# Two token tiles taken together in the mixing stage of a two-layer hybrid decoder trunk

## The chip, the cores and the metric

The kernel runs on one core of a Trainium2 chip. The metric is the device time of one launch in microseconds; a time is given as the median of several runs. A profiled execution of the same program gives a trace: when each instruction started on each engine, and what it waited for. The engines are TensorE (PE in the rows; its weight loads are PEld), VectorE (DVE), ScalarE (ACT), GpSimd (POOL) and SyncE (SP, which issues transfers).

## The reference

The input `x` has 256 tokens of width 1024. Two layers follow each other, each of this form:

```
h    = rms_norm(x, attn_norm)
proj = h @ w_in                       # 1024 x 3218
# split into three groups of heads, all causal:
#  retention: 6 heads of 64, rope on q and k, decay matrix in chunks of 128,
#             rms_norm per head, times silu(gate)
#  sparse attention: 6 query heads on 2 key/value heads, three branches:
#     compressed: 15 blocks of 32 tokens, every 16 tokens:
#         flat   = (tokens of the block + cmp_pe).reshape(32 * 64)
#         k_cmp  = rms_norm(gelu(flat_k @ cmp_w1[0]) @ cmp_w2[0])
#         v_cmp  = gelu(flat_v @ cmp_w1[1]) @ cmp_w2[1]
#     selected blocks, and a window; each branch has softmax with a T5 bias
#     and a sigmoid gate
#  gating: gelu, rms_norm per head, a causal 128 x 128 product over tokens
x = x + concat(heads) @ w_out
h = rms_norm(x, ffn_norm)
x = x + (silu(h @ w_gate) * (h @ w_up)) @ w_down       # inner width 2816
```

Everything is float32. The part that matters here is the per-head work between `proj` and `w_out`, and in it the compressed branch: for keys and for values, on 2 heads, a first layer that contracts 32 positions x 64 channels into 64, a GELU, and a second layer of 64 x 64.

## The kernel before

**Tiles.** The 256 tokens are two tiles of 128 (`t` = 0, 1), with tokens on the partitions. Weights stream from memory in pieces of up to 128 x 1024 (`PIECES`), in the order of use. Each fp32 product of the large matrices is made from three products: `stream_hi` has ACT cast a piece to a high half (`whi`), `stream_lo` has DVE subtract it to get a low half (`wlo`), and PE multiplies high by high, high by low and low by high. Activations are split in the same way after a transpose on PE (`hcat`, `Kh`/`Kl`, `Q`, and others).

**Stages of a layer.** `project` multiplies by the seven column chunks of `w_in` in the order `ORDER` (nk, nq, gm, nv, rq, rk, rg), and forks for each a handler `mix_nk`, `mix_nq` and so on, which works on the two result banks, one per token tile. `residual` multiplies by `w_out`; `project` and `project_t` make the FFN's first layer in chunks; `residual` again makes the second.

**Order of the work.** `Desk` is a planner that runs while the program is built. Handlers are generators: each yields an instruction with an engine, waits for events, or asks for a buffer from a pool (`w2k`: six of 128 x 512, `w1k`: four of 128 x 256, `sm` and `acc`: four PSUM banks each). The planner holds a time for each engine and a cost for each instruction (`_cost_PE`, `_cost_DVE`, `_cost_ACT`, `_cost_POOL`), takes the next by readiness and priority, and so fixes the order of every engine's queue. On the chip each engine runs its queue in that order, and waits on semaphores where a result is not there. A list of instructions that a handler yields at once stays together in the queue.

**The parts that the change touches.** `head_rms` computes per-head sums of squares of one tile and `rsqrt` their inverse root by small DVE operations (with `newton_only` eleven of them, otherwise two ACT functions and three DVE operations). `nk_tile`, `nq_tile`, `gm_tile` and `ret_norm` do this for each tile apart. `keys_twice` writes the normalized keys twice next to each other, `keys` turns them on PE (two transposes per tile) and splits them into `Kh` and `Kl`. `qk_transposed` turns the retention's queries and keys, one tile at a time. `ffn_first` turns the FFN's first chunk, two transposes per tile, and `row_scale` has one matmul per tile.

For the compressed branch `cmp_dup` writes the tokens twice next to each other, so that a transpose gives 128 partitions with the same 64 channels twice (two transposes per tile, and for keys and values apart); `cmp_tokens` has DVE copy even and odd positions to the lower and the upper 64 partitions of `aT`. `compress` then makes the first layer from 16 pairs of positions, for keys and for values, with 128 rows each:

```
PE.matmul(ph[64*j : 64*j+64, :33], self.w1[:, j, a, :], self.aT[:, j, a : a+257 : 8], ...)
for a in range(16) for j in range(2)
```

Here the weights (64 columns) stand in the array and 33 columns stream: 32 blocks, and a 33rd column with the position encoding `cmp_pe`, whose product is added to the others afterwards. After the GELU two products with `w2` follow apart from each other (`pv`, then `pk`). `load_layer` issues the loads of `w1`, `w2` and others on SP's queue; `ev_cmp` tells `compress` that they are there.

Of the kernel before, what the change touches and what calls it, by code (L numbers as in the profile page):

```python
# [22 lines left out]
NB = 384  # L23
# [132 lines left out]
FIRST, SLOT, GRAIN = 16512, 32, 512  # L156
# [33 lines left out]
class Engine:  # L190
# [209 lines left out]
class Trunk:  # L400
    def __init__(self, ctx, tc, x, wts, cst, oh, relb, par, w1, w2, wsT, out):
# [19 lines left out]
        self.pad(FIRST)  # L421
# [25 lines left out]
    def pad(self, first):  # L447

        gap = -(first + self.kept) % GRAIN
        if gap:  # L450
            self.fixed(f"pad{self.kept}", [128, gap // 4])
# [10 lines left out]
    def rsqrt(self, a, name, newton_only=False):  # L462
# [4 lines left out]
        z = self.tiny(name + "_z", shape)  # L467
        if newton_only:
            i = self.tiny(name + "_i", shape, I32)
            yield V.tensor_single_scalar(i, a.bitcast(I32), 1, op=ALU.logical_shift_right)  # L470
            yield V.tensor_scalar(y.bitcast(I32), i, -1.0, float(0x5F3759DF), op0=ALU.mult, op1=ALU.add)
        else:
            yield A.activation(z, a, AF.Ln)
            yield A.activation(y, z, AF.Exp, scale=-0.5)
        for _ in range(3 if newton_only else 1):
            yield V.scalar_tensor_tensor(z, y, -0.5, y, op0=ALU.mult, op1=ALU.mult)
            yield V.tensor_tensor(z, z, a, op=ALU.mult)
            yield V.scalar_tensor_tensor(y, z, 1.5, y, op0=ALU.add, op1=ALU.mult)
# [75 lines left out]
    def setup(self):  # L554
# [15 lines left out]
        self.w2 = self.fixed("w2", [128, 64])  # L570
        self.ev_cst, self.ev_bias, self.ev_scr = Event(), Event(), Event()
# [42 lines left out]
    def load_layer(self, l):  # L614
        SP, G = self.SP, self.G
        if l:
# [4 lines left out]
        w1 = lambda j: SP.dma_start(  # L621
            self.w1[:, j], self.d["w1"][l].rearrange("p (j a e) -> p j a e", j=2, a=16)[:, j], lat=False
        )
# [6 lines left out]
        if l:  # L630
# [4 lines left out]
            self.desk.fire(self.ev_cmp[l])  # L635
            yield causal()
            self.desk.fire(self.ev_lay[l])
            return
# [15 lines left out]
        self.desk.fire(self.ev_cmp[l])  # L654
        yield self.loaded[16]
        yield SP.dma_start(self.cst[:, C_DEC:], self.d["cst"][:, C_DEC:])
        self.desk.fire(self.ev_dec)

    def setup_bias(self):
# [7 lines left out]
        wide = self.tiny("rbw", [33, 6, n])  # L667
# [5 lines left out]
        yield PE.matmul(ps[: 6 * n, :NB], wide.rearrange("p h c -> p (h c)"), oh[:33, :NB], start=True, stop=True)  # L673
# [132 lines left out]
    def norm_scale(self):  # L806
# [21 lines left out]
        for op in ops:  # L828
            op.dur = self.desk.LAT["DVE"]
        yield ops  # L830
# [3 lines left out]
    def head_rms(self, src, nh, name, eps, newton_only=False):  # L834
        sq = yield Need(self.w2k)
        sv = sq[:, : nh * 64].rearrange("p (h d) -> p h d", h=nh)
        yield self.A.activation(sv, src, AF.Square)
        ss = self.tiny(name + "_ss", [128, nh])
        yield self.V.tensor_reduce(ss, sv, axis=AX.X, op=ALU.add)
        self.desk.give(self.w2k, sq)  # L840
        yield self.V.tensor_scalar(ss, ss, 1.0 / 64, eps, op0=ALU.mult, op1=ALU.add)
        r = yield from self.rsqrt(ss, name, newton_only)
        return r
# [9 lines left out]
    def mix_gm(self, l, ps):  # L853
        self.vn = self.gmv.rearrange("p (g t d) -> p t g d", g=4, t=2)
        both = [Event(), Event()]
        for t in range(2):
            self.desk.fork(self.gm_tile(l, t, ps[t], both[t]), 30)
        self.desk.fork(self.gm_mix(l, both), 30)

    def gm_tile(self, l, t, ps, ready):  # L860
        V, A, give = self.V, self.A, self.desk.give
        yield self.rready[t]
        self.z[t] = yield Need(self.w2k)
        z = self.z[t]
        yield A.activation(z, ps, AF.Gelu_apprx_tanh, scale=self.rstd[t])
        give(self.acc, ps)
        zv = self.heads(z[:, 256:], 4)
        r = yield from self.head_rms(zv, 4, f"gmr{t}", EPS, newton_only=True)
        yield V.tensor_tensor(self.vn[:, t], zv, r[:, :, None].to_broadcast([128, 4, 64]), op=ALU.mult)
        self.desk.fire(ready)  # L870
# [42 lines left out]
    def mix_nq(self, l, ps):  # L913
        for t in range(2):
            self.desk.fork(self.nq_tile(l, t, ps[t]), 10)

    def nq_tile(self, l, t, ps):
        V, A, give = self.V, self.A, self.desk.give
        yield self.rready[t]
        src = self.heads(ps, 8)  # L920
        r = yield from self.head_rms(src, 8, f"nqr{t}", self.axe[t])
        nn = yield Need(self.w2k)
        q = nn[:, :384]
        yield V.tensor_tensor(
            self.heads(q, 6), self.heads(ps[:, :384], 6), r[:, :6, None].to_broadcast([128, 6, 64]), op=ALU.mult
        )
        kk = yield from self.keys_twice(ps[:, 384:], r[:, 6:])
        give(self.acc, ps)
        pt = yield Need(self.sm)
        yield [self.transpose(pt[:, j * 128 : j * 128 + 128], q[:, j * 128 : j * 128 + 128]) for j in range(3)]  # L930
        give(self.w2k, nn)
# [3 lines left out]
        for g in range(2):  # L935
# [3 lines left out]
            yield A.activation(hi, src, AF.Copy, scale=self.qg[up])  # L939
            yield V.scalar_tensor_tensor(  # L940
                self.Q[low, hs, ts], src, self.qg[up], hi.bitcast(F32), op0=ALU.mult, op1=ALU.subtract
            )
        give(self.sm, pt)
        yield from self.keys(kk, 0, t)
        self.desk.fire(self.ev_nq[t])

    def keys_twice(self, src, r):
        kk = yield Need(self.w1k)
        yield self.V.tensor_tensor(
            kk.rearrange("p (g r d) -> p g r d", g=2, r=2),  # L950
# [3 lines left out]
        return kk  # L954

    def keys(self, kk, b, t):
        pt = yield Need(self.sm)
        yield [self.transpose(pt[:, g * 128 : g * 128 + 128], kk[:, g * 128 : g * 128 + 128]) for g in range(2)]
        self.desk.give(self.w1k, kk)
        src, gain = pt[:, :256].rearrange("p (g n) -> p g n", g=2), self.par[:, P_KG + 1 + b : P_KG + 2 + b]  # L960
        hi, lo = (k[:, :, b, t * 128 : t * 128 + 128] for k in (self.Kh, self.Kl))
# [4 lines left out]
    def mix_nk(self, l, ps):  # L966
        for t in range(2):
            left = [2]
            self.desk.fork(self.nk_tile(l, t, ps[t], left), 10)
            self.desk.fork(self.nk_rest(l, t, ps[t], left), 12)  # L970
# [6 lines left out]
    def nk_tile(self, l, t, ps, left):  # L977
        V, A, give = self.V, self.A, self.desk.give
        yield self.rready[t]
        src = self.heads(ps[:, :128], 2)  # L980
        r = yield from self.head_rms(src, 2, f"nkr{t}", self.axe[t])
        kk = yield from self.keys_twice(ps[:, :128], r)
        self.part_done(ps, left)
        yield from self.keys(kk, 1, t)
        self.desk.fire(self.ev_nk[t])

    def nk_rest(self, l, t, ps, left):
        yield self.rready[t]
        dup = yield from self.cmp_dup(ps[:, 384:512], t)
# [3 lines left out]
        yield from self.cmp_tokens(dup, 0, t)  # L993

    def cmp_dup(self, src, t):
        dup = yield Need(self.w1k)
        d4 = dup.rearrange("p (g r d) -> p g r d", g=2, r=2)
        yield [
# [851 lines left out]
```

## Time and profile before

| | |
|---|---|
| time, median of 3 runs | 630.7 us (630.62 to 630.87) |
| profiled execution | 630.12 us, of it span 628.3 us |
| PE busy | 623.6 us, 3628 instructions |
| DVE busy | 448.1 us, 976 instructions |
| ACT busy | 367.3 us, 685 instructions |
| POOL busy | 11.8 us, 25 instructions |
| granted TensorE clock | 0.999 |

The span runs from the first to the last instruction of the core; the profiled execution's own time is 1.8 us longer. PE busy time is the union of matmuls whose ends are modelled: a matmul's row can show 0.39 us while the next starts 0.23 us after it. So a cost on PE is read from start to start. Layer 0's mixing runs from about 26 to 110 us, layer 1's from about 330 to 418. A row of the timeline has the start in us, the length in us, the engine, the operation, the tile written and those read, the shapes, and how many instructions were merged into it. A row of a group by line ends with busy us, mean ns of one, idle us before them and what ended it. A row of a stretch has the busy us of PE, PEld, DVE, ACT and POOL with their counts, the granted clock, and the share and the rate of transfers.

### The profile page before, as it was taken

The numbers are of one execution on the slowest core, as the hardware profiler recorded it, in microseconds if no ns is written. First come the engines' busy times: TensorE is split into PE (matmuls) and PEld (weight loads), VectorE is DVE, ScalarE is ACT, GpSimd is POOL, SyncE is SP. The second block draws the span as 40 slices with busy tenths as digits, with TensorE's granted clock in tenths as the row PEclk, the third lists the DMA queues.
The fourth block names the chain that finished last, engine by engine and source line by source line (L and its number), as shares of the span: only waits on it lengthen the run. The fifth ranks groups of instructions, "written<-read, shape, count | busy, mean of one in ns | idle before, by whom it ended". The sixth has DMA issues, their size and how long they took to land.

```text
span 628.3 us, 9870 instructions
## 1 busy us (share of the span) xinstructions
PE 623.6 (99%) x3628; PEld 534.0 (85%) x3628; DVE 448.1 (71%) x976; ACT 367.3 (58%) x685; POOL 11.8 (2%) x25
## 2 busy tenths in 40 slices
PE   9999999999999999999999999999999999999998
PEld 7888788888898888888888978888889898888886
DVE  5988997685668586854388899867847777676432
ACT  6869854575555555544368885546755565555330
POOL 1120000000000000200000000000000000000000
PEclk9999999999999999999999999999999999999999
DMA  8884254355646556785356523545554656657631
GB/s 314 294 274 156 75 160 158 110 171 168 206 163 213 189 171 205 242 271 186 87 168 212 195 71 98 169 135 167 191 178 150 213 173 195 207 168 230 203 103 67
DMA packets 33887, 111.62 MB, mean 178 GB/s; under 512 B 4323, under 2 KB 5603, under 8 KB 33840
## 3 DMA queue, kind: packets, MB, share of 16 engines
q1 hardware_dynamic: 33520, 110.62, 54.0%
q8 instruction: 28, 0.46, 0.3%
q0 software_dynamic: 176, 0.36, 0.2%
q14 instruction: 19, 0.16, 0.1%
q10 hardware_dynamic: 144, 0.03, 0.0%
HBM read 109.64 MB, written 1.35 MB: 177 GB/s over the span
## 4 chain that ended last, share of the span: by engine, by line
PE 98%; DMA 1%; SPq 0%; ACT 0%; DVE 0%; issue 0%
PE acc L203 69%; PE sm L203 29%; DMA wst<-in_wts_dram 1%; SPq L203 0%; ACT whi L203 0%; DVE x L203 0%
## 5 line engine op out<-in xcount | busy, mean ns | idle before, releaser
L203 ACT CAST whi<-wst 128x1024 fp32r<-128x1024 f32 (+3 forms) x198 | 201.6, 1022 | 160.8 <-DMA wst<-in_wts_dram 97.0
L203 DVE TENSOR_TENSOR wlo<-wst,whi 128x1024 fp32r<-128x1024 f32 (+3 forms) x198 | 232.7, 1186 | 78.1 <-ACT whi L203 67.5
L203 PE MATMUL acc<-whi,hcat 128*128 128x512 f32 (+2 forms) x512 | 141.8, 380 | 0.1
L203 PEld LDWEIGHTS acc<-whi,hcat 128*128 128x128 f32 x512 | 91.3, 188 | 14.6 <-ACT whi L203 0.5
L203 PE MATMUL acc<-hcat,whi 128*128 128x512 f32 x320 | 99.4, 391 | 0.0
L203 PE MATMUL sm<-hcat,whi 128*128 128x512 f32 x320 | 98.8, 390 | 0.0
L203 PE MATMUL acc<-wlo,hcat 128*128 128x512 f32 (+2 forms) x256 | 79.4, 377 | 0.0
L203 PEld LDWEIGHTS sm<-hcat,whi 128*128 128x128 f32 x320 | 59.9, 188 | 12.6
L203 PEld LDWEIGHTS acc<-hcat,whi 128*128 128x128 f32 x320 | 58.9, 188 | 11.1
L203 PE MATMUL sm<-hcat,wlo 128*128 128x256 f32 x320 | 64.5, 283 | 0.0
L203 PE MATMUL acc<-hcat,wlo 128*128 128x256 f32 x320 | 64.3, 283 | 0.0
L203 PEld LDWEIGHTS acc<-wlo,hcat 128*128 128x128 f32 x256 | 46.8, 188 | 7.7 <-ACT hcat L203 0.6
L203 PEld LDWEIGHTS acc<-hcat,wlo 128*128 128x128 f32 x320 | 51.2, 191 | 1.6
L203 PE MATMUL acc<-whi,ah 128*128 128x512 f32 (+1 forms) x176 | 50.0, 378 | 0.0
L203 PE MATMUL acc<-whi,al 128*128 128x512 f32 (+1 forms) x176 | 50.0, 378 | 0.0
L203 DVE TENSOR_TENSOR w2k<-sm,w2k 128x256 f32<-128x256 f32 x40 | 16.9, 423 | 46.3 <-ACT w2k L203 46.3
L203 PE MATMUL acc<-wlo,ah 128*128 128x512 f32 (+1 forms) x176 | 49.9, 377 | 0.0
L203 PEld LDWEIGHTS sm<-hcat,wlo 128*128 128x128 f32 x320 | 49.9, 192 | 0.0
L203 PEld LDWEIGHTS acc<-whi,al 128*128 128x128 f32 x176 | 31.8, 188 | 5.6
L203 PEld LDWEIGHTS acc<-wlo,ah 128*128 128x128 f32 x176 | 31.8, 188 | 5.5
L203 PEld LDWEIGHTS acc<-whi,ah 128*128 128x128 f32 x176 | 31.7, 188 | 5.4
L203 ACT ACTIVATE hcat<-sm,par 128x128 fp32r<-128x128 f32 (+1 forms) x60 | 18.0, 384 | 10.1 <-PE sm L203 10.1
(213 smaller groups left out, 726.6 us busy)
## 6 DMA issues: line engine op xcount, KB each, us to landing
wst<-in_wts_dram SPq DMA_DIRECT2D x177, 512.0 KB, 4.2
PT<-in_wts_dram SPq DMA_DIRECT2D x7, 512.0 KB, 7.1
wst<-in_wts_dram SPq DMA_DIRECT2D x8, 384.0 KB, 3.0
w<-in_w_dram SPq DMA_DIRECT2D x4, 512.0 KB, 7.7
wst<-in_wts_dram SPq DMA_DIRECT2D x7, 256.0 KB, 2.9
wst<-in_wts_dram SPq DMA_DIRECT2D x4, 411.0 KB, 6.3
x<-in_x_dram SPq DMA_DIRECT2D x4, 256.0 KB, 5.2
B<-scr SPq DMA_DIRECT2D x4, 192.0 KB, 3.7
```

The lines of the kernel that those rows point to most:

```text
L203: return Op(self.name, lambda: fn(*a, **k), dur, table, lat, prio, banks)
```

## The change

Both token tiles go through the small operations together, and the compressed branch's first layer is laid out anew.

- `head_rms` takes both tiles: it makes sums for both into one small tile, and `rsqrt` works on both at once. `chain` yields small DVE operations as one list.
- `nk_tiles`, `nq_tiles`, `gm_tiles` and `ret_norm` replace the versions per tile. `keys` turns both tiles with four transposes in one list into one bank and splits them by one ACT and one DVE operation. `qk_transposed` turns four blocks at a time, two of each tile. `ffn_first` yields its four transposes as one list, `row_scale` its two matmuls.
- The tokens of the compressed branch are no longer written twice: one transpose per tile, two ACT copies for both tiles, and `aT` holds keys in the lower and values in the upper 64 partitions, with the 512 positions of both heads side by side. The first layer goes by single positions: tokens (32 blocks) stand in the array, `w1` (64 columns) streams; keys use the lower 64 rows, values the upper, and four neighbouring positions go to four groups of 32 output partitions. The four partial sums are turned by one more transpose and added by a DVE reduction.
- The position encoding's product is made by POOL (`position_sums`): products of `w1` and `cmp_pe` in four rounds, folded by additions into a 64-column row `pw`, which two more matmuls with a tile of ones add in. POOL holds a `w2k` buffer in each round.
- The two products of the second layer are yielded as one list. `w1` is loaded by four transfers of half the size. The planner's cost of a large matmul is 0.4167 n + 13.3 ns in place of 0.422 n (at n = 512, 227 in place of 216 ns), and a 32-partition, 64-column matmul is entered with 16 ns.

```diff
-            return max(0.422 * n, load + 27), None
+            return max(0.4167 * n + 13.3, load + 27), None
...
+        if a[0].shape[0] == 32 and n == 64:
+            return 16, None
...
+    def position_sums(self, l):
+
+        G = self.G
+        if l == 0:
+            yield G.memset(self.ones, 1.0)
+        for j in range(2):
+            for r in range(2):
+                yield G.tensor_copy(
+                    self.pe[64 * j : 64 * j + 64, r], self.par[64 * r : 64 * r + 64, P_PE + 16 * j : P_PE + 16 * j + 16]
+                )
+        for r in range(2):
+            for a in (0, 8):
+                buf = yield Need(self.w2k)
+                yield G.tensor_tensor(
+                    buf.rearrange("p (a e) -> p a e", a=8), self.w1[:, r, a : a + 8, :],
+                    self.pe[:, r, a : a + 8, None].to_broadcast([128, 8, 64]), op=ALU.mult,
+                )
+                yield G.tensor_tensor(buf[:, :256], buf[:, :256], buf[:, 256:], op=ALU.add)
+                yield G.tensor_tensor(buf[:, :128], buf[:, :128], buf[:, 128:256], op=ALU.add)
+                if r or a:
+                    yield G.tensor_tensor(buf[:, :64], buf[:, :64], buf[:, 64:128], op=ALU.add)
+                    yield G.tensor_tensor(self.pw, self.pw, buf[:, :64], op=ALU.add)
+                else:
+                    yield G.tensor_tensor(self.pw, buf[:, :64], buf[:, 64:128], op=ALU.add)
+                self.desk.give(self.w2k, buf)
+        self.desk.fire(self.ev_cmp[l])
...
-    def keys(self, kk, b, t):
+    def keys(self, kk, b):
+
         pt = yield Need(self.sm)
-        yield [self.transpose(pt[:, g * 128 : g * 128 + 128], kk[:, g * 128 : g * 128 + 128]) for g in range(2)]
+        p4 = pt.rearrange("p (g t n) -> p t g n", g=2, t=2)
+        yield [
+            self.transpose(p4[:, t, g], kk[:, 256 * t + 128 * g : 256 * t + 128 * g + 128]) for t in range(2) for g in range(2)
+        ]
...
-    def nk_tile(self, l, t, ps, left):
-        yield self.rready[t]
...
+    def nk_tiles(self, l, ps, left):
+        for t in range(2):
+            yield self.rready[t]
+        r = yield from self.head_rms(lambda t: self.heads(ps[t][:, :128], 2), 2, "nkr")
+        kk = yield Need(self.w2k)
+        for t in range(2):
+            yield self.keys_twice(kk, t, ps[t][:, :128], r[:, t])
+            self.part_done(ps[t], left[t])
+        yield from self.keys(kk, 1)
...
+    def cmp_tokens(self, raw, j, t):
+
+        if t == 0:
+            self.tok[j] = yield Need(self.sm)
+            self.desk.fire(self.ev_pt[j])
+        yield self.ev_pt[j]
+        pt = self.tok[j]
+        yield self.transpose(pt[:, t * 128 : t * 128 + 128], raw[:, :128])
+        self.desk.give(self.w1k, raw)
+        self.toks[j] += 1
+        if self.toks[j] == 2:
+            yield [
+                self.A.copy(self.aT[64 * j : 64 * j + 64, 256 * g : 256 * g + 256], pt[64 * g : 64 * g + 64, :256])
+                for g in range(2)
+            ]
...
         yield [
-            PE.matmul(
-                ph[64 * j : 64 * j + 64, :33], self.w1[:, j, a, :], self.aT[:, j, a : a + 257 : 8],
-                start=a == 0, stop=a == 15,
-            )
-            for a in range(16)
-            for j in range(2)
...
+        for n in range(0, 32, 4):
+            for q in range(4):
+                for j in range(2):
+                    rows, p = slice(64 * j, 64 * j + 64), n + q
+                    ops.append(
+                        PE.matmul(
+                            ph[j][32 * q : 32 * q + 32, :64], self.aT[rows, p : p + 497 : 16],
+                            self.w1[rows, p % 2, p // 2, :], start=n == 0, stop=n == 28 and q > 0,
+                        )
+                    )
+        for j in range(2):
+            rows = slice(64 * j, 64 * j + 64)
+            ops.append(PE.matmul(ph[j][:32, :64], self.ones[rows, :], self.pw[rows, :], start=False, stop=True))
+        yield ops
+        cw = yield Need(self.w1k)
+        for j in range(2):
+            yield A.copy(cw[:, 64 * j : 64 * j + 64], ph[j][:, :64])
+            give(self.sm, ph[j])
+        pt = yield Need(self.sm)
+        yield self.transpose(pt[:, :128], cw[:, :128])
```

More of the change, by code (lines that the diff above doesn't have):

```diff
@@ L672, in setup_bias @@
         ps = yield Need(self.sm)
-        yield PE.matmul(ps[: 6 * n, :NB], wide.rearrange("p h c -> p (h c)"), oh[:33, :NB], start=True, stop=True)
+        yield PE.matmul(ps[: 6 * n, :NB], room[:33, : 6 * n], oh[:33, :NB], start=True, stop=True)
+        self.desk.give(self.w1k, room)
         yield self.A.copy(ext[: 6 * n, :NB], ps[: 6 * n, :NB])
@@ L913, in mix_nq, with nq_tiles, queries @@
     def mix_nq(self, l, ps):
+        self.desk.fork(self.nq_tiles(l, ps), 10)
+    def nq_tiles(self, l, ps):
+        V, give = self.V, self.desk.give
         for t in range(2):
[L915 to L928, printed above, removed]
+            yield self.rready[t]
+        r = yield from self.head_rms(lambda t: self.heads(ps[t], 8), 8, "nqr")
+        kk = yield Need(self.w2k)
+        go = []
+        for t in range(2):
+            nn = yield Need(self.w2k)
+            yield V.tensor_tensor(
+                self.heads(nn[:, :384], 6), self.heads(ps[t][:, :384], 6),
+                r[:, t, :6, None].to_broadcast([128, 6, 64]), op=ALU.mult,
+            )
+            yield self.keys_twice(kk, t, ps[t][:, 384:], r[:, t, 6:])
+            give(self.acc, ps[t])
+            go.append(Event())
+            self.desk.fork(self.queries(l, t, nn, go[t]))
+        yield from self.keys(kk, 0)
+        for t in range(2):
+            yield go[t]
+            self.desk.fire(self.ev_nq[t])
+    def queries(self, l, t, nn, ready):
         pt = yield Need(self.sm)
-        yield [self.transpose(pt[:, j * 128 : j * 128 + 128], q[:, j * 128 : j * 128 + 128]) for j in range(3)]
-        give(self.w2k, nn)
+        yield [self.transpose(pt[:, j * 128 : j * 128 + 128], nn[:, j * 128 : j * 128 + 128]) for j in range(3)]
+        self.desk.give(self.w2k, nn)
         ts = slice(t * 128, t * 128 + 128)
@@ L1670, in row_scale @@
             yield self.rready[t]
-            yield self.PE.matmul(
+        yield [
+            self.PE.matmul(
                 ps[:, t * 128 : t * 128 + 128], self.rstd[t].to_broadcast([128, 128]), self.ident, start=True, stop=True
             )
+            for t in range(2)
+        ]
         yield self.A.copy(self.rbc, ps[:, :T])
@@ L1692, in tile @@
             give(self.w1k, sg)
-            yield [self.transpose(p4[:, k, t, :], act[:, k * 128 : k * 128 + 128]) for k in range(2)]
-            give(self.w1k, act)
-            left[0] -= 1
-            if left[0] == 0:
-                self.desk.fire(both)
+            acts[t] = act
+            self.desk.fire(both[t])
         for t in range(2):
             self.desk.fork(tile(t))
-        yield both
+        for t in range(2):
+            yield both[t]
+        yield [
+            self.transpose(p4[:, k, t, :], acts[t][:, k * 128 : k * 128 + 128]) for t in range(2) for k in range(2)
+        ]
+        for t in range(2):
+            give(self.w1k, acts[t])
         yield from self.split(h, lo, pt.rearrange("p (k n) -> p k n", k=2))
@@ L1794, in main @@
             pool.__exit__(None, None, None)
-        self.pad(FIRST)
+        self.pad(512)
 def trunk_kernel(tc, *args):
```

302 lines of the change are left out of this document (165 added, 137 removed).

## The prediction

> **What bounds the kernel now.** I read the page first: busy time by engine, then the chain that ended last.
>
> ```profile
> span 628.3 us, 9870 instructions
> PE 623.6 (99%) x3628; PEld 534.0 (85%) x3628; DVE 448.1 (71%) x976; ACT 367.3 (58%) x685; POOL 11.8 (2%) x25
> ...
> PE 98%; DMA 1%; SPq 0%; ACT 0%; DVE 0%; issue 0%
> ...
> L203 DVE TENSOR_TENSOR wlo<-wst,whi 128x1024 fp32r<-128x1024 f32 (+3 forms) x198 | 232.7, 1186 | 78.1 <-ACT whi L203 67.5
> ```
>
> TensorE (PE) is busy 99% of the span and makes 98% of the chain. (The row of `wlo`, the low halves of the weights, is used below.) A busy share can hide waits, because matmul ends are modelled, so I next asked for all waits of PE, which gave one row, and for stages of layer 0's mixing.
>
> ```profile
> PE acc L203 <- DVE w2k L203: 1.4, 1, 1.4
> ```
>
> ```profile
> 40.00:50.00 10.00, 10.00 (x70) 9.35 (x69) 6.94 (x12) 8.26 (x14) 0.00 (x0) 1.00 0.88 265
> 50.00:60.00 10.00, 10.00 (x91) 8.50 (x89) 9.96 (x56) 9.98 (x33) 0.00 (x0) 1.00 0.36 119
> 60.00:80.00 20.00, 20.00 (x129) 16.25 (x126) 18.91 (x85) 16.31 (x48) 0.00 (x0) 1.00 0.28 89
> ```
>
> The only wait is 1.4 us at the very start (the first warm-up matmul). So the time is a sum of PE start-to-start intervals: an instruction taken from PE is worth its interval, and one added costs it. The stages add a warning. From 50 to 60 us DVE (9.96 of 10) and ACT (9.98) are as full as PE, so there PE lives on work prepared earlier.
>
> **The change, part by part.** All costs are PE start-to-start intervals out of the timeline. A 512-wide matmul among its own kind takes 0.23 us, by the longest piece of the chain (52.84 us for 233); the second piece below is layer 1's compressed branch.
>
> ```profile
> 255.84 52.84 PE acc L203 x233
> ...
> 363.81 2.15 PE sm L203 x64
> ```
>
> *Transposes.* One pair and one group of four:
>
> ```profile
> 54.72 0.38 PE L203 MATMUL sm<-cst,w1k 128*128 128x128 f32 x2
> 54.86 0.48 PE L203 MATMUL acc<-wlo,hcat 128*128 128x512 f32 x1
> 55.18 0.38 PE L203 MATMUL sm<-cst,w1k 128*128 128x128 f32 x2
> ...
> 128.35 0.60 PE L203 MATMUL sm<-cst,x 128*128 128x128 f32 x4
> 128.70 0.48 PE L203 MATMUL acc<-whi,rtl 128*128 128x512 f32 x1
> 129.02 0.39 PE L203 MATMUL acc<-whi,rth 128*128 128x512 f32 x1
> ```
>
> The pair holds PE 0.14 us (54.72 to 54.86) and stretches the next matmul from 0.23 to 0.32 (54.86 to 55.18): 0.23 in all. The four hold it 0.35 and stretch the next by 0.09: 0.44. So a transpose costs 0.11, and what a group adds is only about 0.02. Per layer the change drops four transposes (the compressed branch's tokens are no longer written twice before turning): -0.44. It adds one, of the compressed hidden layer: +0.12 with its group. It joins groups at five places (keys twice, the retention's queries and keys, the FFN's first chunk, the row scale's two matmuls): -0.10.
>
> *Second layer of the compressed branch.* Its two small products stand apart now:
>
> ```profile
> 68.56 0.38 PE L203 MATMUL sm<-w,hg 64*96 64x64 f32 x2
> 68.86 0.50 PE L203 MATMUL acc<-whi,hcat 128*128 128x512 f32 x1
> ...
> 69.66 0.39 PE L203 MATMUL acc<-whi,hcat 128*128 128x512 f32 x1
> 69.97 0.30 PE L203 MATMUL sm<-w,hg 64*32 64x64 f32 x2
> 70.20 0.50 PE L203 MATMUL acc<-wlo,hcat 128*128 128x512 f32 x1
> 70.54 1.03 PE L203 MATMUL sm<-cst,S 128*128 128x128 f32 x8
> ```
>
> The second of them stretches the matmul ahead (69.66 to 69.97, 0.31 for 0.23) and the one behind (70.20 to 70.54, 0.34). Issued together they pay this once: 0.08 + 0.11, so -0.20 per layer.
>
> *First layer of the compressed branch*, the largest term and the unknown one:
>
> ```profile
> 58.39 0.39 PE L203 MATMUL acc<-whi,hcat 128*128 128x512 f32 x1
> 58.71 2.23 PE L203 MATMUL sm<-aT,w 128*64 128x33 f32 x64
> 60.86 0.51 PE L203 MATMUL acc<-whi,hcat 128*128 128x512 f32 x1
> ...
> 99.97 1.58 PE L203 MATMUL sm<-qkT 64*128 64x256 f32 x16
> 101.48 0.44 PE L203 MATMUL acc<-whi,hcat 128*128 128x384 f32 x1
> ...
> 105.59 1.62 PE L203 MATMUL sm<-rv,S 128*64 128x64 f32 x48
> 107.14 0.73 PE L203 MATMUL acc<-whi,gmh 128*128 128x512 f32 x2
> ```
>
> Now 32 calls (64 passes; an fp32 matmul shows as two) take 2.15 us: 0.034 a pass, 0.067 per two calls. The retention's sums, also with 64 columns of the array, take 1.55 us for 48 passes, 0.032 each; the scores, on 64 rows, 1.51 us for eight 256-wide and eight 128-wide passes, which alone at a transpose's 0.108 per 128 columns would take 2.6. So two matmuls on different halves of the array, by columns or by rows, overlap. The new form has 66 calls, 132 passes, each on 64 rows and 32 columns with 64 streamed: eight such tiles fill the array, two row halves by four column quarters. No row shows eight overlapping. Bounds: if all eight run as the two do now, a group of eight calls takes 2 x 0.067 = 0.13 us, and nine groups (the last is the two bias calls) 1.2, or 1.3 with the way out. If only two ever overlap, 132 x 0.034 = 4.5 us. I take 1.35, near the lower bound, because both kinds of overlap are shown separately and nothing in the rows ties them: -0.80 per layer (ends -0.85 and +2.35).
>
> The Trainium skill speaks against this. *TensorE: Matmul & The Clock Gate*, section "Wait — 56ns, not 53.3ns?", says that two matmuls never start less than about 25 ns apart however small they are. By it the first layer would take 132 x 0.025 = 3.3 us, +1.15 per layer. The 0.032 us of the rows above lies above that floor and does not refute it.
>
> *POOL and the queues.* The position encoding's product moves from PE's 33rd column to POOL: per layer 4 small copies and 19 arithmetic operations, reading `w1` once it has landed, ahead of the first layer. In layer 0 `w1` is issued at 25.94 and lands about 37:
>
> ```profile
> 25.94 2.64 SPq L203 DMA_DIRECT2D w<-in_w_dram  x3
> ...
> 268.47 0.42 SPq L203 DMA_DIRECT2D w<-in_w_dram  x1
> ```
>
> ```profile
> DMA to landing us min/median/max: 8.7/9.6/10.1
> ```
>
> The next rows show POOL and DVE together in layer 1, and then the `wlo` group of DVE from 37 to 58 us:
>
> ```profile
> 263.94 1.29 POOL L203 TENSOR_TENSOR wsT<-wsT,cst 128x512 f32<-128x512 f32 x1 [4.54 <-DMA wsT<-in_wsT_dram]
> 264.29 2.02 DVE L203 TENSOR_TENSOR wlo<-wst,whi 128x1024 fp32r<-128x1024 f32 x1 [0.25 <-ACT whi L203]
> 265.17 1.21 POOL L203 COPY aT<-par 128x32 f32<-128x32 f32 x1
> ```
>
> ```profile
> L203 DVE TENSOR_TENSOR wlo<-wst,whi 128x1024 fp32r<-128x1024 f32 (+2 forms) x7 | 7.8, 1120 | 0.3 <-ACT whi L203 0.3
> ```
>
> A 512-wide POOL product takes 1.29 us. With halves at 0.7, 0.4 and two of 0.25 (estimates in proportion to it) four rounds are some 11.5, and 12.5 with the copies: done at about 50, against 58.7 for its user. The middle row shows a cost: a `wlo` subtraction, 1.19 us on average by the page, took 2.02 while POOL worked, and the 32-wide copy behind it took 1.21. They shut each other out. The Trainium skill (*SBUF — State Buffer*, "Who interferes with whom") has it as a lock between POOL and a DVE instruction with two inputs in SBUF; by that the trace agrees. Seven `wlo` subtractions, 7.8 us, fall between 37 and 58 us, so POOL may finish anywhere from 50 to 58, or later if other DVE work adds to it. I cost it at nothing, because the 58.7 covers most of that; without the cover every microsecond past it is one of PE's. DVE loses up to 12 us to POOL there, but 40 to 50 us has 3 us free. In layer 1 `w1` is issued by 268.5 and its user stands at 363.8. The two more `w1` issues on SP's queue (four of half the size) fall ahead of a free stretch.
>
> *DVE and ACT* are off PE's path and costed at nothing:
>
> ```profile
> L203 DVE COPY aT<-sm 64x128 f32<-64x128 f32 x16 | 4.0, 281 | 0.7 <-PE sm L203 0.5
> L203 DVE SCALAR_TENSOR_TENSOR gmr_y<-gmr_z,gmr_y 128x4 f32<-128x4 f32 x12 | 1.8, 150 | 0.0
> ```
>
> Eight token copies leave DVE (8 x 0.281 = 2.2 us) and about 26 operations on a few columns go, since both tiles share them (26 x 0.15 = 3.9): 6 us per layer in the fullest stage. It pays for much of POOL's lock.
>
> *Waits.* Queries, keys, norms and gating of tile 0 now wait for tile 1's sums. Queued behind are transposes and scores on PE; other weights' matmuls stand between. The planner, too, gets 0.227 in place of 0.216 for a 512-wide matmul and lays everything out anew. I add 0.4 us for small new waits (bounds 0 and 3; PE's one wait today is 1.4).
>
> **Sum.** Per layer -0.44 + 0.12 - 0.10 - 0.20 - 0.80 = -1.42; two layers -2.8; with the waits -2.4. Against the profiled execution's own 630.1 us (span 628.3 and 1.8 around it) that is 627.7; the median of the runs is 630.7, so **628.3**, 0.4% faster.
>
> **Rivals.**
>
> (a) *A pass keeps its price.* If only two tiles overlap, or a pass has a price of issue near today's 0.032 to 0.034, the first layer takes 4.2 to 4.5 us, 2.9 to 3.1 per layer more than forecast: 634.1 to 634.5, slower. If four overlap, 2.2 us in place of 1.35: 630.0, no change. The change loses once a pass takes more than about 0.02 us on average (1.35 + 1.2 = 2.55 us over 132). For it: no row goes below 0.032, and none has 64 x 32 tiles; against: halves overlap both ways. The floor of the page named above would put the time between the two, at 632.2.
>
> (b) *POOL is late in layer 0*, and PE, in order, stands at the first layer. For it: the lock. Against: 8 us of cover. With 2.5 us late: 630.8.
>
> (c) *PE's gain is hidden anyway*: between 50 and 80 us DVE and ACT are full, and PE reaches their results sooner and waits. Against: PE does not wait today, and DVE loses 6 us of work. What is left is some 0.5 us: 630.2.
>
> **How the numbers follow.** Forecast 0.52, with its own range 626.6 to 629.6; (a) today's price per pass, whole or in good part, 0.14, four at a time 0.10; (b) 0.14; (c) 0.10. Runs of this kernel can tell about 0.2% (1.3 us) from no change. Faster (below 629.4): the forecast nearly whole, and a part of (b) and (c): 0.58. Slower (above 632): the dear part of (a) and the long tail of (b): 0.18. Same: 0.24. The range leaves out today's full price per pass and the best corner: 626.6 to 632.4.
>
> **What would show it.** The first layer's 132 passes: about 1.3 us between their start and the next matmul's (right), 2.2 or more (a). Transposes: 0.11 each, and six fewer over the kernel. POOL's last operation of layer 0 before 58 us, and no wait of PE for POOL (else b). PE still without waits of more than 0.5 us (else c). A PE that drops 2.8 us of intervals while the time stays would make the prediction wrong.

## The result, and the profile after

The changed kernel takes **639.01 us** (median; 638.6 to 640.7) beside 630.66 us (630.2 to 630.9) for the kernel before on the same chip: a ratio of 1.0141, 95% interval 1.0127 to 1.0155. It is slower by 8.35 us, where 2.4 us less was forecast, and it lies outside the range.

The page of the changed kernel, busy time and the chain that ended last (as shown of before):

```profile
span 637.5 us, 10109 instructions
PE 624.1 (98%) x3758; PEld 530.6 (83%) x3758; DVE 446.6 (70%) x902; ACT 368.2 (58%) x671; POOL 48.4 (8%) x72
...
PE 81%; DVE 8%; DMA 4%; ACT 4%; issue 2%; SPq 0%; ACTq 0%; DVEq 0%
```

PE's busy time is nearly what it was (623.6 before), and the span is 9.2 us longer: PE now stands idle. DVE, ACT and transfers, next to nothing of the chain before, make 16% of it. All waits of PE in the changed kernel (us in total, how many, the longest):

```profile
PE acc L203 <- DVE w2k L203: 3.0, 2, 1.6
PE sm L203 <- DVE amx L203: 1.5, 1, 1.5
PE sm L203 <- DVE rstd L203: 1.3, 2, 0.7
PE sm L203 <- DMA x<-in_x_dram: 0.8, 2, 0.4
PE sm L203 <- DVE x L203: 0.8, 2, 0.5
PE sm L203 <- DVE w2k L203: 0.8, 1, 0.8
PE sm L203 <- ACT w1k L203: 0.8, 1, 0.8
PE sm L203 <- ACT S L203: 0.4, 1, 0.4
PE sm L203 <- DVE gmv L203: 0.2, 1, 0.2
```

Before, this view had one row of 1.4 us. Now it has nine, in nearly every stage of both layers and even in the feed-forward part, which the change hardly touches. They add up to 9.6 us. Counted in another way, as every PE start-to-start interval that exceeds the usual one of its shape by 0.08 us or more, the excess is 13.9 us where before had 3.3: 10.6 more. The span grew by 9.2, so by this count some 1.4 us of PE work was saved and 10.6 us of waiting was added. What is called usual moves such a count by some tenths: with the usual interval taken from a matmul's shape and that of the one ahead of it, and without the first 10 us, the excess is 13.8 against 3.6, that is 10.2 more.

**Was the work saved where it was foretold?** The first layer of the compressed branch in the changed kernel, layer 0 (the row of 124 is most of its 132 passes, the last one its end):

```profile
57.60 1.59 PE L203 MATMUL sm<-w,aT 64*32 64x64 f32 x124
...
59.18 0.96 PE L203 MATMUL acc<-whi,hcat 128*128 128x512 f32 x3
```

From 57.60 to 59.18 it takes 1.58 us, where before took 2.15, so 0.012 us a pass. Layer 1 takes the same 1.58.

**Where a wait comes from.** The largest in layer 0's mixing stands ahead of the transposes of the compressed branch's tokens. Rows of PE, then of DVE, ACT and POOL in the same stretch of the changed kernel:

```profile
52.78 0.63 PE L203 MATMUL acc<-whi,hcat 128*128 128x512 f32 x2
54.93 0.30 PE L203 MATMUL sm<-cst,w1k 128*128 128x128 f32 x1 [1.52 <-DVE amx L203]
```

```profile
49.77 3.21 DVE L203 TENSOR_TENSOR wlo<-wst,whi 128x1024 fp32r<-128x1024 f32 x2 [1.03 <-ACT whi L203]
52.90 0.20 DVE L203 TENSOR_SCALAR negr<-rstd 128x1 f32<-128x1 f32 x2
53.02 0.67 DVE L203 TENSOR_REDUCE gmr_ss<-w2k 128x8 f32<-128x512 f32 x1
53.73 0.38 DVE L203 TENSOR_SCALAR gx<-acc,negr 128x18 f32<-128x18 f32 x2
```

```profile
54.00 0.62 ACT L203 ACTIVATE w1k<-acc,rstd 128x128 f32<-128x128 f32 x2 [1.75 <-DVE gx L203]
```

```profile
49.81 2.08 POOL L203 TENSOR_TENSOR w2k<-w,pe 128x512 f32<-128x512 f32 x1
```

PE (52.78 plus two matmuls) is ready for the transposes at about 53.2. They read `w1k`, which ACT makes, and ACT had waited 1.75 us for `gx` of DVE; the row of PE names `amx`, a DVE result that follows `gx` in DVE's queue. Either way DVE had come late out of two `wlo` subtractions. These took 3.21 us, where two take 2.35 in a row below, while POOL worked on the position sums. Whether POOL's work is what makes the kernel slower is tested further down.

The wait in the feed-forward part (changed kernel, PE and then DVE):

```profile
262.88 0.61 PE L203 MATMUL acc<-whi,al 128*128 128x512 f32 x2
265.05 0.83 PE L203 MATMUL acc<-whi,ah 128*128 128x512 f32 x2 [1.55 <-DVE w2k L203]
```

```profile
262.31 2.35 DVE L203 TENSOR_TENSOR wlo<-wst,whi 128x1024 fp32r<-128x1024 f32 x2
264.58 0.75 DVE L203 TENSOR_TENSOR w2k<-acc,w2k 128x256 f32<-128x256 f32 x2
```

No POOL work is near. DVE simply has two `wlo` subtractions in its queue ahead of the operations that empty PE's bank. The queue's order is the planner's, so the question became why it lays the order so.

Two prices of the planner changed with the code. A large matmul went from 0.422 n (216 ns at n = 512) to 0.4167 n + 13.3 (227). In the lists of small dependent DVE operations that `chain` makes, an operation is entered with 80 ns, where the row scale's list had 150 before; `rsqrt`'s operations, yielded one by one before, each had the planner's DVE latency of 150 ns behind them (some 220 ns a step, with the 69 to 75 that the planner enters for the operation itself), and are now 80 ns each in one list. What the chip makes of such a list can be read at the row scale of the changed kernel (first operation and `rstd`, then PE's wait):

```profile
140.38 0.15 DVE L203 TENSOR_TENSOR nr_a<-ss 128x2 f32<-128x2 f32 x1
...
142.54 0.16 DVE L203 TENSOR_TENSOR nr_z<-nr_z,nr_a 128x2 f32<-128x2 f32 x1
142.74 0.16 DVE L203 SCALAR_TENSOR_TENSOR rstd<-nr_z,nr_y 128x2 f32<-128x2 f32 x1
```

```profile
141.67 0.61 PE L203 MATMUL acc<-whi,hcat 128*128 128x512 f32 x2
142.95 0.38 PE L203 MATMUL sm<-cst,rstd 128*128 128x128 f32 x1 [0.67 <-DVE rstd L203]
```

Thirteen operations up to `rstd` take 140.38 to 142.90, that is 2.52 us, 0.20 from one start to the next, because each needs the one before. The planner's sum for the list's fourteen at 80 ns and one latency is 14 x 0.08 + 0.15 = 1.27 us; at 150 ns it is 2.25. So at 80 it has the row scale ready 1.25 us too early, puts PE's use of it there, and PE stands (from about 142.12). The same place before, where the list was priced at 150 (DVE, then PE):

```profile
139.95 0.16 DVE L203 TENSOR_TENSOR nr_z<-nr_z,nr_a 128x2 f32<-128x2 f32 x1
140.15 0.16 DVE L203 SCALAR_TENSOR_TENSOR rstd<-nr_z,nr_y 128x2 f32<-128x2 f32 x1
```

```profile
140.89 0.38 PE L203 MATMUL sm<-cst,rstd 128*128 128x128 f32 x2
```

There the operations start 0.20 us apart as well; `rstd` was done at 140.31 and PE came 0.58 us later.

### The profile page after: what moved, and what is told of

Its sections match the earlier page's. It is cut to its first block, busy times and chain, and to the rows that moved or that the text cites. A ratio compares the mean times of both kernels' runs of the same rounds, so it can differ in the third digit from the quotient of the medians.

```text
span 637.5 us, 10109 instructions
## 1 busy us (share of the span) xinstructions
PE 624.1 (98%) x3758; PEld 530.6 (83%) x3758; DVE 446.6 (70%) x902; ACT 368.2 (58%) x671; POOL 48.4 (8%) x72
## 3 DMA queue, kind: packets, MB, share of 16 engines
HBM read 109.64 MB, written 1.35 MB: 174 GB/s over the span
## 4 chain that ended last, share of the span: by engine, by line
PE 81%; DVE 8%; DMA 4%; ACT 4%; issue 2%; SPq 0%; ACTq 0%; DVEq 0%
PE acc L203 54%; PE sm L203 27%; DMA wst<-in_wts_dram 4%; DVE wlo L203 3%; ACT whi L203 2%; DVE hcat L203 1%; DVE S L203 1%; DVE x L203 1%; ACT w2k L203 1%; DVE nr_z L203 0%; ACT hcat L203 0%; SPq L203 0%; DVE hu L203 0%; DVE w1k L203 0%; DVE nr_y L203 0%
## 5 line engine op out<-in xcount | busy, mean ns | idle before, releaser
L203 DVE TENSOR_TENSOR wlo<-wst,whi 128x1024 fp32r<-128x1024 f32 (+3 forms) x198 | 234.3, 1198 | 87.2 <-ACT whi L203 81.7
L203 PE MATMUL acc<-whi,hcat 128*128 128x512 f32 (+2 forms) x512 | 136.2, 378 | 0.1
L203 ACT CAST ah<-w2k 128x512 fp32r<-128x512 f32 x20 | 12.4, 621 | 22.1 <-DVE w2k L203 22.1
```

Of the source, the lines that this page charges most:

```text
L203: return Op(self.name, lambda: fn(*a, **k), dur, table, lat, prio, banks)
```

## The experiments

**The theories.** (1) The planner's two changed prices make the waits: the matmul's, or the chain's, or both together. (2) POOL's position sums hold DVE up. (3) The joined code itself is late: lists of DVE operations that can't be interleaved, and tiles that wait for each other. Ratios below are to the kernel before on the same chip, with their 95% intervals. A number at a wait that comes without a row is a PE start-to-start excess as counted above.

**The matmul's price undone, alone.**

```diff
-            return max(0.4167 * n + 13.3, load + 27), None
+            return max(0.422 * n, load + 27), None
```

> The changed kernel, with the planner's cost of a large matmul set back to 0.422 n (216 ns at 512 columns); nothing that is computed changes, only the order on the engines. PE of the changed kernel has 10.6 us more of waits than PE of the kernel before. Theory M (the truer matmul cost makes the planner lay PE close behind DVE and ACT): the waits go almost all, 629 to 632 us. Theory C (the small DVE chains are entered at 80 ns an operation and take 150): the waits behind chains stay, 635 to 640 us. Theory P (POOL's position sums lock DVE out): 636 to 640 us.

634.1 us, ratio 1.0061 (1.0044 to 1.0078). PE's waits with the row scale shrink, but stay:

```profile
PE acc L203 <- DVE w2k L203: 1.7, 2, 1.5
PE sm L203 <- issue: 1.0, 1, 1.0
PE sm L203 <- DVE rstd L203: 0.5, 2, 0.2
```

That is 4.0 us above the kernel before, where the changed kernel was 8.35 above it: 4.3 us are gained.

**The chain's price undone, alone.**

```diff
-            op.dur = max(op.dur, 80)
+            op.dur = max(op.dur, 150)
```

> The changed kernel, with the operations of a chain entered in the planner at 150 ns in place of 80. Theory C: the waits before the row scale's matmuls (0.83 us in each layer), before the transposes of queries and keys in layer 1 (0.9 and 0.9) and before the gating's product (0.4 and 0.35) go, some 4.5 us: 634 to 635.5 us. Theory M: they come from the matmul cost and stay: 637.5 to 640. Theory P: the same, 637.5 to 640.

637.7 us, ratio 1.0109 (1.0078 to 1.0141). Its profiled execution was the fastest of its four, 634.9 us. No wait for `rstd` is left in it, but others take their place (1.5 us before `x` is turned at 128 us, 1.4 in layer 0's keys). It is 7.6 us above the kernel before, so alone this is worth 0.7 us, which the intervals don't tell from nothing. (The row scale's list had 150 before; for `rsqrt`'s operations 150 is still less than the 220 of before.)

**The position sums taken away, the prices left as in the changed kernel.** `position_sums` keeps only its event, and `pw` is zero: the position encoding is left out of the result.

> The changed kernel without the position encoding's products on POOL: POOL writes zeros to the row once and computes nothing more, so the position encoding is left out of the compressed branch. POOL then works about 10 us in place of 48. Theory P: the 1.7 us wait at 53 us goes, and with DVE undisturbed from 36 to 55 us and in layer 1 most of the others too: 630 to 634 us. Theories M and C: only the wait at 53 us goes, 636.5 to 638.5 us.

639.0 us, ratio 1.0133 (1.0114 to 1.0152): no change. Its waits:

```profile
PE sm L203 <- DVE w2k L203: 2.5, 3, 1.1
...
PE sm L203 <- DVE rstd L203: 1.3, 2, 0.7
```

POOL's lock on DVE is real: without it the `wlo` group's mean falls from 1198 to 1183 ns. At the place of the wait of 1.52 us shown above 0.77 is left (at 56 us), and other waits stand elsewhere (0.9 and 1.1 us at 41 and 44). So POOL has a part in single waits, but it isn't the cause of the slowdown.

**The matmul's new price in the kernel before.** The same line as in the first edit, the other way round, and nothing else of the change.

> The kernel before, with only the planner's cost of a large matmul changed to 0.4167 n + 13.3 ns. Theory M: PE gets waits of the same kind without any other part of the change, 634 to 641 us. Theories C and P: 630 to 632 us, no change.

632.3 us, ratio 1.0030 (1.0018 to 1.0041): the price alone costs 2.2 us in a kernel in which no instruction was changed.

**Both prices undone.** The two edits above together, on the changed kernel.

> The changed kernel with both planner costs set back at once: 0.422 n for a large matmul and 150 ns for each operation of a chain. Alone the first left 4.0 us above the kernel before and the second 7.6. If the two costs together explain the loss, PE's waits fall to what the kernel before has and its 2 to 2.5 us of saved work show: 627.5 to 629.5 us. If POOL's lock or the joining of the tiles itself makes the rest, 631 to 635 us.

**629.5 us**, ratio 0.9986 (0.9977 to 0.9996). It is 0.8 us below the kernel before. The two edits were worth 4.3 and 0.7 us one by one; together they are worth 9.2. The page and all of PE's waits of this kernel:

```profile
span 628.1 us, 10089 instructions
PE 621.9 (99%) x3758; PEld 531.8 (85%) x3758; DVE 445.6 (71%) x902; ACT 368.1 (59%) x671; POOL 48.0 (8%) x72
...
PE 98%; DMA 1%; DVE 1%; ACT 0%; issue 0%; ACTq 0%
```

```profile
PE acc L203 <- DVE w2k L203: 1.5, 1, 1.5
PE sm L203 <- DVE w2k L203: 1.0, 1, 1.0
```

The instructions' work is that of the changed kernel. PE makes 98% of the chain again, and 50 to 60 us is full. The stretch in the changed kernel, and then in this one:

```profile
50.00:60.00 10.00, 8.48 (x172) 6.99 (x171) 9.77 (x46) 8.17 (x24) 4.64 (x6) 1.00 0.41 132
```

```profile
50.00:60.00 10.00, 10.00 (x177) 8.42 (x177) 9.65 (x50) 9.87 (x32) 4.43 (x8) 1.00 0.49 160
```

At the row scale PE again has other matmuls until `rstd` is there (139.38), and uses it at 139.96:

```profile
139.22 0.16 DVE L203 SCALAR_TENSOR_TENSOR rstd<-nr_z,nr_y 128x2 f32<-128x2 f32 x1
```

```profile
139.96 0.61 PE L203 MATMUL sm<-cst,rstd 128*128 128x128 f32 x4
```

**Both prices undone and the position sums taken away** (the position encoding is left out).

> The same, and POOL's position products left out, with zeros in their place (the position encoding is missing from the compressed branch). Theory P: at least 1.5 us below the run with both costs. Otherwise within 1 us of it.

630.3 us, ratio 1.0000 (0.9990 to 1.0009). With neither set of prices do the sums cost anything that can be measured; the second theory falls.

**The compressed branch's part alone**, in the kernel before: first layer by single positions, tokens not doubled, position sums on POOL, `w1` in four loads, second layer's products in one list; keys, queries, gating and norms stay per tile, and prices as before but for the new small matmul's.

```diff
+        if a[0].shape[0] == 32 and n == 64:
+            return 16, None
...
-        dup = yield from self.cmp_dup(ps[:, 384:512], t)
+        raw = yield from self.cmp_scaled(ps[:, 384:512], t)
```

> The kernel before with only the compressed branch's part of the change: single positions, tokens written once, position sums on POOL, four loads of w1. Query, key, gating and norm work stays tile by tile, the planner's matmul cost stays 0.422 n. The saved PE work (first layer 0.6 to 0.8 us a layer, transposes 0.3, second layer 0.2) is 2.2 to 2.6 us in two layers. If the joined tiles and the costs make all the waits: 627.5 to 629 us. Theory P: waits near 50 to 60 us eat it, 630 to 633 us.

631.5 us, ratio 1.0015 (1.0004 to 1.0026). The shorter first layer is there, and waits of 1.1, 0.6, 1.1 and 1.6 us (at 6, 54, 106 and 371 us) eat it.

**Wide margins.** On the kernel with both prices undone, the planner's latencies are raised.

```diff
-    LAT = {"PE": 170, "DVE": 150, "ACT": 190, "POOL": 200, "DMA": 2000, "SWDMA": 4500}
+    LAT = {"PE": 250, "DVE": 250, "ACT": 290, "POOL": 300, "DMA": 2000, "SWDMA": 4500}
```

> The changed kernel with both costs set back, and the planner's latencies raised (PE 170 to 250, DVE 150 to 250, ACT 190 to 290, POOL 200 to 300 ns), so that it places what follows a result later. If PE's waits come from plans that are too tight, they shrink further, 627 to 629.5 us. If they come from too much work on DVE and ACT ahead of PE, they stay or grow, 631 to 637 us.

638.1 us, ratio 1.0115 (1.0098 to 1.0132). More caution in every latency doesn't remove the waits: 1.9 us at 44 us and 1.3 each at 124 and 433 us are new.

**Truer prices for the chain.** 200 ns is what the row scale shows. First with the old matmul price, then with the new one, which is also what the chip takes (0.227 us, by the prediction's longest piece).

```diff
-            op.dur = max(op.dur, 80)
+            op.dur = max(op.dur, 200)
```

> The changed kernel with the matmul cost set back to 0.422 n and 200 ns for each operation of a chain, which is what the changed kernel's trace shows between dependent operations on DVE (60.10, 60.30, 60.50, 60.70, 60.90 us). With 150 ns it took 629.5 us and PE had two waits left, 1.2 and 0.3 us, both before transposes of queries and keys that follow a chain. If the price of a chain is what is left, these go: 628 to 629.2 us. If not, 629 to 631.

> The changed kernel as it is, with 200 ns for each operation of a chain: both prices are now what the trace shows (227 ns for a large matmul, 200 for a chained operation). If only the chain's price was wrong, the waits go: 628 to 630.5 us. If the truer matmul price alone brings PE too close, because everything else around it is priced low, waits of 3 us or more stay: 632 to 637 us.

634.4 us, ratio 1.0066 (1.0046 to 1.0086), and 633.1 us, ratio 1.0047 (1.0029 to 1.0065): both are worse than 629.5. A plan in which these two prices are true isn't the best plan here. With both of them the waits move to layer 0's keys and queries (rows of its slowest execution, 637.0 us):

```profile
33.29 0.44 PE L203 MATMUL sm<-cst,w2k 128*128 128x128 f32 x2 [1.60 <-DVE w2k L203]
35.09 0.69 PE L203 MATMUL sm<-cst,w2k 128*128 128x128 f32 x2 [1.36 <-DVE w2k L203]
35.42 2.06 PE L203 MATMUL acc<-whi,hcat 128*128 128x512 f32 x4
37.28 1.05 PE L203 MATMUL acc<-wlo,hcat 128*128 128x512 f32 x2
```

**No lists in `rsqrt`.** Both prices undone, and `rsqrt` yields its operations one by one again, so that each has the price of before, some 220 ns a step. The lists of the row scale and of the compressed branch's hidden layer stay, at 150.

```diff
-        yield self.chain(*ops)
+        for op in ops:
+            yield op
```

> The changed kernel with the matmul cost 0.422 n, and the root's small operations yielded one by one as in the kernel before, so that DVE can do other work between them (the scale of the norms and the hidden layer's chains stay lists at 150 ns). If a list costs DVE time that PE later waits for, this is faster than the run with both costs set back (629.5 us): 627.5 to 629 us. If the lists cost nothing, 629 to 631.5.

630.1 us, ratio 0.9995 (0.9987 to 1.0004). 629.5 with the list at 150 ns is no worse, so joining `rsqrt`'s operations into a list costs nothing that can be seen. A step near 200 ns isn't bad in itself either: here 220 gives 630.1, where 200 for every list gave 634.4.

**The chain's new price in the kernel before**, for the row scale, its only list of this kind.

```diff
-            op.dur = self.desk.LAT["DVE"]
+            op.dur = max(op.dur, 80)
```

> The kernel before, with only the norm's chain of 14 operations entered at 80 in place of 150 ns. Theory C: the row scale's matmuls are placed too early and PE waits there 0.8 us in each layer, as in the changed kernel: 631.5 to 633 us. Otherwise 630 to 631 us, no change.

631.8 us, ratio 1.0022 (1.0014 to 1.0031), 1.6 us more, and the wait for the row scale appears in both layers:

```profile
PE sm L203 <- DVE rstd L203: 0.5, 2, 0.2
```

**Nudges.** 639 and 629.5 could still be two draws: any change of a price makes the planner lay another order. So the prices were moved by half a nanosecond at n = 512: 0.4167 n + 12.8 and + 13.8 in the changed kernel, 0.421 n and 0.423 n in the one with both prices undone. Each lays PE's queue anew in many places.

> After's kernel, with one price nudged: a large matmul is entered with 0.4167 n + 12.8 ns in place of + 13.3 (226.2 for 226.7 ns at n = 512). The instructions are the same, the planner lays them out anew (its order differs from after's in many places). Theory L (the slowdown is a property of the order that these prices happen to give; any other order is another draw): the time moves by more than 1 us to either side, anywhere from 629 to 640. Theory W (the price of 227 is wrong in itself, with chain operations at 80: PE is thought too slow, so work is planned too late): the price is nearly the same, so the time stays at 639 within 1 us.

> After's kernel with 0.4167 n + 13.8 ns (227.2 at n = 512), the other way. Theory L: anywhere from 629 to 640, and not tied to the direction of the nudge. Theory W: 639 within 1 us, or a little above.

> The kernel both_costs (large matmul 0.422 n, chain operations 150 ns), with 0.421 n (215.6 for 216.1 ns at n = 512). Theory L: 629.5 was a good draw, so this is slower, by 1 to 5 us. Theory W: 629.5 within 1 us.

> The kernel both_costs with 0.423 n (216.6 ns at n = 512). Theory L: slower than 629.5 by 1 to 5 us. Theory W: 629.5 within 1 us.

640.4 and 638.3 us (ratios 1.0165, 1.0145 to 1.0185; 1.0114, 1.0094 to 1.0135), against 630.2 and 629.4 us (1.0001, 0.9990 to 1.0012; 0.9983, 0.9974 to 0.9993). Neighbouring orders scatter by about 1 us either way, three on each side, so the 9 us are no such draw: they go with the sizes of the prices. The waits are others each time, of the same kind. Those of the nudge down in the changed kernel begin:

```profile
PE sm L203 <- DVE w2k L203: 3.5, 3, 2.3
PE acc L203 <- DVE w2k L203: 2.9, 2, 1.5
PE sm L203 <- DVE rstd L203: 1.3, 2, 0.7
```

The wait for `rstd`, 1.3 us in two, is the one that stays to the digit; the wait in the feed-forward part is there again too, with 1.6 us (1.0 in the nudge up).

**A matmul price lower still.** 0.405 n (207 ns), with the chain at 80 and at 150.

> After's kernel with one price changed: a large matmul is entered with 0.405 n (207 ns at n = 512; after has 227, before had 216), chain operations stay at 80. Theory M (a matmul price below the measured 227 to 230 ns is slack: on the chip PE is late against the plan, so the other engines' results are there; what counts is how much slack there is): 207 gives more of it than 216, so the time falls below the 634.1 of 216 with 80, to 629.5 to 632.5. Theory F (216 is no slack but the value that the other prices fit; any other value misplaces work): 634 or more.

> The kernel both_costs (0.422 n, chain 150) with 0.405 n (207 ns at n = 512). Theory M: no wait is left to gain much from, so 628.5 to 630.5. Theory F: 631.5 or more, with waits of PE in places where there were none.

632.4 us, ratio 1.0036 (1.0024 to 1.0049), and 633.9 us, ratio 1.0051 (1.0037 to 1.0066). With the chain at 80 the time falls with the matmul price (639.0, 634.1, 632.4 at 227, 216, 207; the intervals of the last two touch). With the chain at 150 it doesn't: 637.7, 629.5, 633.9, with a new wait of 2.6 us:

```profile
PE sm L203 <- DVE w1k L203: 2.8, 2, 2.6
```

In seven of that kernel's eight runs the granted clock is 0.995 to 0.997 as well, and they took 633.6 to 635.2 us; the one at 1.000 took 631.5. Neither of the expectations' two theories (M and F) holds for both kernels. All pairs of these prices tried on the changed instructions, median us (on several chips, on which the kernel before took 630.1 to 630.7):

| matmul at n = 512 | chain 80 | chain 150 | chain 200 |
|---|---|---|---|
| 207 ns | 632.4 | 633.9 | |
| 216 ns | 634.1 | **629.5** | 634.4 |
| 227 ns | **639.0** | 637.7 | 633.1 |

## Why the prediction was wrong

**The PE side was right in kind and less in size.** Of the terms, the first layer was set at 1.35 us and measured 1.58 in both layers, so -0.57 per layer instead of -0.80. With the other terms as forecast (-0.62 per layer) the two layers give -2.4 instead of -2.8. PE's instructions fit too: 130 more, which is 136 more passes of the first layers less six transposes. The other terms were not timed one by one. The intervals without excess bear out 1.4 us of the saving in the changed kernel (9.2 - 10.6) and 2.2 in the one with both prices undone (625.0 before, that is 628.3 - 3.3, against 628.1 - 5.3 = 622.8); by the second way of counting it is 1.0 and 2.0 (5.4 us of excess there). These are differences of large sums. So the change does save PE's work, by 1 to 2 us.

**Rival (a) fell.** Tiles of 64 x 32 overlap far better than two at a time: 0.012 us a pass, where the price before was 0.032 to 0.034; the first layer's 1.58 us lies between the 1.35 taken for eight at a time and the 2.2 for four. The floor of about 25 ns between two matmul starts, from the Trainium skill (*TensorE: Matmul & The Clock Gate*, section "Wait — 56ns, not 53.3ns?"), would have made 3.3 us of these 132 passes. The trace has 1.58, so it doesn't hold for matmuls on different tiles of the array.

**Rival (b) fell.** POOL's last sum of layer 0 started at 54.58 and ended before the first layer at 57.60:

```profile
54.58 0.32 POOL L203 TENSOR_TENSOR pw<-pw,w2k 128x64 f32<-128x64 f32 x1
```

The forecast's lock was there, and the runs without the sums show that it costs the kernel no time that can be measured.

**The step that failed is the one on waits**: "The planner, too, gets 0.227 in place of 0.216 for a 512-wide matmul and lays everything out anew. I add 0.4 us for small new waits (bounds 0 and 3; PE's one wait today is 1.4)." What was measured is 10.6 us (10.2 by the second count), some three and a half times its upper bound. It stands nearest to rival (c), PE waiting for DVE and ACT, but not by (c)'s mechanism. That one had PE reach full engines sooner and lose at most its gain, between 50 and 80 us; here waits arise everywhere, up to the feed-forward part, and most go when two numbers of the planner are put back while the code stays.

Three things were overlooked in that step. First, it read that PE does not wait before as a property of the kernel. It was a property of an order, and the price of 216 ns for what takes 227 was part of it: putting 227 into the kernel before costs 2.2 us. Second, it did not look at the price of 80 ns in `chain` at all, nor did it see that the same step of `rsqrt` had been priced at some 220. The trace of before had the evidence: the row scale's operations start 0.20 us apart there too. The price I took for such an operation on DVE was its duration, 0.15, which says nothing of when the next one that needs it can start. Third, "DVE and ACT are off PE's path and costed at nothing" holds only as long as the order keeps them early. DVE lost little, moreover: 448.1 to 446.6 us busy, 1.5 in all, where 6 per layer were forecast less POOL's lock.

**How the two prices act** is shown at the row scale. With 80 and 227 PE waits there 0.83 us in each layer. With 80 and 216 it waits 0.38, and with 80 and 216 in the kernel before 0.39; with 80 and 207 no wait for `rstd` is left, and with 150 there is none, at any matmul price. The list's price is short by 1.25 us against the chip at 80 and by 0.27 at 150. That a matmul price below the real one is slack, since PE then comes to each place later than planned, agrees with these numbers. As a rule for the whole kernel it isn't shown: 207 with 150 and all prices at 200 are worse, and why 216 with 150 is the best of the table stays open. What the runs show is that it is the two prices, by their size and together (both undone, 9.2 us), and not chance (the nudges).

**What the change is worth** with the prices kept: 629.4 to 630.2 us in three orders against 630.3 to 630.4 for before, so 0.1% or nothing. In the profiled executions some 2 us of PE work are saved and nearly as much more of waits taken (5.3 against 3.3), which is why little of it is seen. The best of all runs are this version, with both prices undone, whose interval (0.9977 to 0.9996) lies just below one, and its nudge up, 0.9983 (0.9974 to 0.9993). They are the best of many, and the kernel before was not nudged, so how much its own order is a lucky one stays open.

## What to carry to other kernels

Where a planner fixes the order of the queues, its prices are part of the kernel: a diff that changes a price gets a term of its own in the sum, with a range as wide as all idle time that the order now hides, and is best timed apart from the change of the instructions. A small instruction that needs the one before it costs its start-to-start distance in a dependent run, which the timeline shows, and not its duration. And a price nearer to the chip's need not give a better plan; when the time moves against a right sum, look at the list of waits of the engine that sets the end, and ask of each which queue brought the result late.

## What was not expected of the hardware

Fp32 matmuls of 64 rows by 32 columns with 64 columns streamed ran at 0.012 us a pass when neighbours in the queue went to eight different tiles of the array (132 passes in 1.58 us).

Waits of PE can cost more than they last. In the run with true prices, after the 1.60 and 1.36 us quoted above (3.0 of some 4 us idle), four 512-wide matmuls from 35.42 take 1.86 us to the row at 37.28, that is 0.46 each, twice their usual interval. The clock fell during the second of these waits (0.71 from 34.0 to 34.5 us, then 0.50). The stretches of that run give the granted clock ahead of the last two numbers:

```profile
35.00:41.00 6.00, 5.91 (x15) 4.76 (x16) 5.70 (x12) 3.10 (x6) 2.24 (x4) 0.50 0.87 219
41.00:50.00 9.00, 9.00 (x45) 7.41 (x45) 6.29 (x9) 5.43 (x9) 8.22 (x13) 1.00 0.78 271
```

Half the clock for some 6 us costs about 3 us more (an estimate from these rows), and that was this kernel's slowest run (637.0, mean granted clock 0.994). With 207 and 150 the wait of 2.65 us that ends at 87.76 is followed by a clock of 0.50 from 90 to 92 us. The mean clocks show it elsewhere: with the chain at 150 alone, the two runs of four at a mean clock of 0.996 to 0.997 took 638.7 and 639.2 us, the two at 1.000 took 634.9 and 636.8. So a part of what such waits cost can come by the clock, and the dearer cells of the table hold some of it. It isn't all: one run with true prices at a mean clock of 1.000 took 636.0 us. In the changed kernel it plays no part, since its clock is 0.999 to 1.000 in all runs. The Trainium skill (*TensorE: Matmul & The Clock Gate*, section "What's actually happening") has the clock halved after an idle window of about 3.4 us; in these two traces no single idle time before the fall reached that (1.60 us and a part of the next wait in one, 2.65 and 0.46 in the other).
